# First layer's conditioning weights as the stationary operand in full precision, the input loaded first, modulation in two fused passes

## Chip, cores, metric

One of the cores of a Trainium2 chip runs the program. The metric is the device time of one launch in microseconds (us); the time before is 1392.67 us, the median of three runs (1392.63 to 1394.99).

## The reference, cut to what matters

A two-layer network over 512 latent tokens of 1024 channels, with 256 context tokens. Layer 0 is a bidirectional gated recurrence, layer 1 a convolution module. Both begin with a modulated RMSNorm whose shift and scale come from a conditioning vector:

```python
def _ada(cvec, w, b):                       # w is 1024 x 3072
    m = jax.nn.silu(cvec) @ w + b
    return jnp.split(m, 3, axis=-1)         # shift, scale, gate
def _modulate(x, g, shift, scale):
    return _rmsnorm(x, g) * (1 + scale) + shift
# layer 0
shift, scale, gate = _ada(c, ada_w[0], ada_b[0])
h = _modulate(x, norm_g[0], shift[:, None], scale[:, None])
shift_c, scale_c, gate_c = _ada(c_ctx, ada_w[0], ada_b[0])
hc = _modulate(ctx, norm_g[0], shift_c, scale_c)
y, yc = _hgrn2_mixer(h, hc, ...)            # first step: h @ w_in, hc @ w_in
```

## The kernel before, in words

Channels lie on the 128 partitions, in KD = 8 blocks (`k`), tokens along the free dimension (512 for `x`, 256 for the context). Large products take operands split into a high part in fp32r and a low part that is the rest (`split`, L134 to L142), and sum three products: high by high, high by low, low by high.

The change lies in the start, before the first head's work. `ada_start(jj)` (L144) computes shift and scale for two of the eight blocks of channels, for the latent and the context vector at once (two columns: `sc`, `sc4`). Each of the four calls takes four pieces of weights `ada{jj}_{kk}` of 128x2x512. As the table `ADA_SPLIT` (L36) says, a piece is either split (high part on ScalarE, low part on VectorE or GpSimd) and multiplied in fp32r, or multiplied whole in fp32. Here the vector is the stationary operand (2 or 4 columns) and the weights stream past it, 512 columns to a matmul (L150, L154, L156). The sums are rows `ps[0:4]`; they are copied (`adarow`, L158) and turned into columns by four small matmuls against `sel` (L161), and then `mod_s` and `mod_g` are made (L164, L165).

`rms_rstd` (L182) squares `x` on ScalarE, adds on VectorE and GpSimd, sums over partitions by a matmul with ones (L195) and gives the reciprocal root `rs`. Then `xn = x*rs` (L262) and `modulate` (L200): high part on ScalarE, the affine form again on VectorE (L202), their difference as the low part (L203). For the context the first multiplication is on GpSimd (L274).

`early_products` (L247) runs 24 matmuls for each of five first weight pieces `we0` to `we4` (L251 to L253, 120 in all), in steps as blocks of `h` come. The next work on TensorE is the product `pc` of the first weight piece with the context (L301).

Loads go on the SP queue in the order of the code (`load`, L90, keeps program order): four pieces of `ada` for each `jj`, `x` behind the first four, the weight pieces between them as `EARLY_LOADS` says, the context with `jj` = 2. The buffers of `ada` pieces (tag `araw`) are 6. In what order each engine issues its instructions is set by a scheduler at build time, from the dependences and an estimate of durations; a matmul of f32 operands stands in the trace as two records with a weight load each.

Of the kernel before, what the change touches and what calls it, by code (L numbers as in the profile page):

```python
# [35 lines left out]
ADA_SPLIT = ((1, 1, 1, 1), (1, 0, 2, 1), (1, 0, 2, 1), (1, 1, 0, 0))  # L36
EARLY, EARLY_LOADS, CTX_AT = 5, (3, 2, 0, 0), 2
# [23 lines left out]
def hybrid_kernel(ctx: ExitStack, tc: tile.TileContext, xT, ctxT, cvec, consts, norm_g, ada_b, ada_a, ada_c,  # L61
# [63 lines left out]
    sc4 = cpool.tile([P, KD, 4], F32R, name="sc4")  # L125
    V.tensor_copy(out=sc4[:, :, 0:2], in_=sc)
    V.tensor_tensor(out=sc4[:, :, 2:4], in0=sc, in1=sc4[:, :, 0:2].bitcast(F32), op=ALU.subtract)

# [15 lines left out]
    def ada_start(jj, raws, pool, sel):  # L144
        ps = ps_m.tile([P, 512], F32, name=f"adaps{jj}", tag="ms")
        n = 4 if ADA_SPLIT[jj][0] else 2
        for kk, raw in enumerate(raws):
            if not ADA_SPLIT[jj][kk]:
                for k in range(2):
                    mm(ps[0:2], lhsT=sc[:, 2 * kk + k, :], rhs=raw[:, k, :], start=(kk == 0 and k == 0), stop=(kk == 3 and k == 1))  # L150
                continue
            hi, lo = split(pool, raw, [2, 512], f"ada{jj}_{kk}", V if ADA_SPLIT[jj][kk] == 1 else G, ("ahi", "alo"), 2)
            for k in range(2):
                mm(ps[0:4], lhsT=sc4[:, 2 * kk + k, :], rhs=hi[:, k, :], start=(kk == 0 and k == 0), stop=False)  # L154
            for k in range(2):
                mm(ps[0:2], lhsT=sc4[:, 2 * kk + k, 0:2], rhs=lo[:, k, :], start=False, stop=(kk == 3 and k == 1))  # L156
        row = pool.tile([4, 512], F32, name=f"adarow{jj}", tag="adarow", bufs=2)
        V.tensor_copy(out=row[0:n], in_=ps[0:n])  # L158
        pt_ = ps_m.tile([P, 512], F32, name=f"adat{jj}", tag="ms")
        for i in range(4):  # L160
            mm(pt_[:, 2 * i:2 * i + 2], lhsT=row[0:n, i * P:(i + 1) * P], rhs=sel[0:n], start=True, stop=True)  # L161
        for i in range(2):
            j = 2 * jj + i
            V.tensor_scalar(out=mod_s[:, j, :], in0=pt_[:, 2 * i:2 * i + 2], scalar1=ab[:, 0, j:j + 1], scalar2=None, op0=ALU.add)  # L164
            V.tensor_scalar(out=mod_g[:, j, :], in0=pt_[:, 4 + 2 * i:6 + 2 * i], scalar1=ab1[:, j:j + 1],  # L165
                            scalar2=ng[:, 0, j:j + 1], op0=ALU.add, op1=ALU.mult)
# [33 lines left out]
    def modulate(t, k, gcol, scol, hi, lo):  # L200
        act(out=hi[k], in_=t, func=AF.Identity, scale=gcol, bias=scol)
        V.tensor_scalar(out=t, in0=t, scalar1=gcol, scalar2=scol, op0=ALU.mult, op1=ALU.add)  # L202
        V.tensor_tensor(out=lo[k], in0=t, in1=hi[k].bitcast(F32), op=ALU.subtract)  # L203
# [6 lines left out]
    # ================= layer 0: bidirectional gated recurrence =================  # L210
    with l0:
# [8 lines left out]
        with tc.tile_pool(name="pinit", bufs=1) as pi:  # L220
            mk = pi.tile([P, 5, P], F32, name="mk")
            eye = pi.tile([4, 4], F32, name="eye")
            nc.gpsimd.dma_start(out=eye, in_=consts[0:4, C_IDN:C_IDN + 4])
            sel = pi.tile([4, 2], F32, name="sel")
            V.tensor_tensor(out=sel, in0=eye[:, 0:2], in1=eye[:, 2:4], op=ALU.add)
            # loads in the order of their use: the vectors' weights, and the first products' between them
            wsrc = [w_in[2, 0, 0], w_in[3, 0, 0], w_in[2, 0, 1], w_in[0, 0, 0], w_in[0, 0, 1]]
            araws, wraws, todo = [], [], list(range(EARLY))
            for jj in range(4):
                araws.append([pi.tile([P, 2, 512], F32, name=f"ada{jj}_{kk}", tag="araw", bufs=6) for kk in range(4)])  # L230
                for kk in range(4):
                    load(araws[jj][kk], ada_a[jj, kk])
                if jj == 0:
                    for i in range(4):
                        load(x_sb[:, 2 * i:2 * i + 2, :], xT[:, 2 * i:2 * i + 2, :])
                for i in todo[:EARLY_LOADS[jj]]:
                    wraws.append(wpool.tile([P, KD, P], F32, name=f"we{i}_raw", tag="raw"))
                    load(wraws[i], wsrc[i])
# [43 lines left out]
            # lower bounds: softmax over the one layer, cumulative sum less the first  # L282
# [46 lines left out]
        def gla(h, j, sg, qs, v):  # L329
# [5 lines left out]
            # cumulative log decays within the chunks, forward and backward  # L335
# [3 lines left out]
            # decays from a context token to the context's end (forward) and start (backward)  # L339
# [16 lines left out]
            # the last head's state and operands lie where the context was  # L356
# [10 lines left out]
            # chunk totals and references; prefix and suffix sums of the totals by level  # L367
# [25 lines left out]
            # block decays  # L393
# [9 lines left out]
            # decayed queries and keys about each chunk's reference  # L403
# [11 lines left out]
            # state terms  # L415
# [21 lines left out]
            # scores by level, both directions at once  # L437
# [45 lines left out]
            # the first product opens the bank, and each later region's first overwrites what it finds  # L483
# [90 lines left out]
        for gi in range(8):  # L574
# [15 lines left out]
            else:  # L590
# [14 lines left out]
                # residual done: its squares and its scaled copy, then the next layer's normalised input  # L605
# [24 lines left out]
                # the transform of the convolution's taps  # L630
# [24 lines left out]
    # ================= layer 1: convolution module =================  # L655
    with ExitStack() as l1:
# [4 lines left out]
        # the convolution's transforms  # L661
# [10 lines left out]
        with tc.tile_pool(name="pu", bufs=1) as pu:  # L672
            for g in range(4):
# [3 lines left out]
                # one row of the grid to a tile: its high part on one half of the partitions, its low part on the other  # L677
# [62 lines left out]
        # LayerNorm over the channels: mean, then the squares about it  # L740
# [23 lines left out]
        # gate path, and the product with it  # L764
# [18 lines left out]
        # residual with the gated bias of the last projection  # L783
# [40 lines left out]
        for mq in range(4):  # L824
            # the last outputs by halves of the tokens, so that the first half is done while the second is summed
# [27 lines left out]
def _constants():  # L853
# [13 lines left out]
    # a depthwise convolution of one row as products between two transforms: the discrete Fourier  # L867
    # transform of NDFT points, in which the row, zeros after it, is as good as padded at both ends
# [9 lines left out]
    # real part p1 - p3, imaginary part p1 + p2  # L878
# [53 lines left out]
```

## Time and profile before

| | |
|---|---|
| median of three runs | 1392.67 us |
| the profiled execution's own span | 1389.6 us (its own time is this span; the runs' median has 3.1 us more around it) |
| TensorE busy | 1332.2 us, 96% of the span |
| VectorE, ScalarE, GpSimd busy | 962.8, 637.4, 368.9 us |
| first matmul of `pc` starts | 77.77 us |
| TensorE busy before that | 61.25 us |
| loads | 115.72 MB on the SP queue |

To read it: rows name engine, source line, operation, output<-inputs and shape. PE is TensorE's matmuls, PEld its weight loads (they run beside matmuls), DVE VectorE, ACT ScalarE, POOL GpSimd, SP the queue that issues loads. Matmuls overlap in their pipeline, so that the time between starts, not the length of a record, tells the pace. PEclk is the TensorE clock granted, as a share of 2.4 GHz; 0.5 is the level of 1.2 GHz.

### The profile page before, as it was taken

The page shows a single profiled execution, that of the slowest core. Times are in us where ns is not written, and L with a number is a line of the kernel's source. Part 1 is how long each engine was busy: PE and PEld are TensorE (multiplying, and loading weights), DVE is VectorE, ACT ScalarE, POOL GpSimd, SP SyncE. Part 2 cuts the span into 40 slices and gives each one's busy share as a digit, 9 for nine tenths or more (in the row PEclk, how much of TensorE's full clock was granted, in tenths as well). Part 3 has the DMA queues.
Part 4 walks back from the last instruction along what each step waited for, and adds up shares of the span by engine and source line. Part 5 has one row for each costly group of instructions (what it writes and reads, how often), then busy time and mean ns, then how long its engine had stood idle before and what let it go on. Part 6 is the DMA issues. An engine that isn't in the chain of part 4 may idle for free.

```text
span 1389.6 us, 18990 instructions
## 1 busy us (share of the span) xinstructions
PE 1332.2 (96%) x7530; PEld 1124.9 (81%) x7530; DVE 962.8 (69%) x1486; ACT 637.4 (46%) x965; POOL 368.9 (27%) x302
## 2 busy tenths in 40 slices
PE   6999999999999999999999999999999999986997
PEld 2588988998888898888898889867787877865887
DVE  8868787896687786787688777756656747278323
ACT  6455553562355354465345455443223333458321
POOL 3222241240240151140033133122211213267221
PEclk9999999999999999999999999999999999998999
DMA  9312113114112312212211312023422322120321
GB/s 361 123 61 77 46 62 107 61 46 146 67 46 64 120 46 88 75 51 92 92 46 47 122 46 75 28 79 106 136 92 91 108 89 92 64 76 28 124 89 61
DMA packets 35720, 119.05 MB, mean 86 GB/s; under 512 B 4562, under 2 KB 6898, under 8 KB 35632
## 3 DMA queue, kind: packets, MB, share of 16 engines
q1 hardware_dynamic: 34960, 115.72, 24.8%
q0 software_dynamic: 672, 2.13, 0.7%
q8 instruction: 59, 0.97, 0.3%
q14 instruction: 29, 0.24, 0.1%
HBM read 115.74 MB, written 2.10 MB: 85 GB/s over the span
## 4 chain that ended last, share of the span: by engine, by line
PE 61%; DVE 22%; ACT 5%; DMA 4%; POOL 4%; issue 3%; SPq 0%; DVEq 0%; ACTq 0%; POOLq 0%
PE pa L688 4%; PE pa L689 4%; PE pa L693 4%; PE pz L301 2%; PE pz L302 2%; PE pz L304 2%; PE pi L728 2%; PE cop L842 2%; PE cop L846 2%; PE cop L843 2%; PE op L530 2%; PE h_sc L465 2%; DVE adacc L176 2%; PE op L532 2%; PE op L531 2%
## 5 line engine op out<-in xcount | busy, mean ns | idle before, releaser
L688 PE MATMUL pa<-ci_hi,h_hi 128*128 128x512 f32 x256 | 99.6, 398 | 1.9 <-ACT h_hi L649 1.9
L689 PE MATMUL pa<-ci_lo,h_hi 128*128 128x512 f32 x256 | 100.4, 396 | 0.0
L116 POOL TENSOR_SCALAR sg<-sg 128x1536 f32<-128x1536 f32 x16 | 76.6, 4787 | 70.7 <-ACT sg L549 70.5
L301 PE MATMUL pz<-h_hi,wz_hi 128*128 128x512 f32 x232 | 93.3, 402 | 0.8 <-ACT wz_hi L139 0.8
L302 PE MATMUL pz<-h_lo,wz_hi 128*128 128x512 f32 x232 | 92.9, 401 | 0.0
L176 DVE SCALAR_TENSOR_TENSOR adacc<-adb,sc,adacc 128x128 f32<-128x128 f32 x224 | 82.0, 384 | 3.6
L141 POOL TENSOR_TENSOR ci_lo<-ci_raw,ci_hi 128x1024 fp32r<-128x1024 f32 x18 | 44.5, 2472 | 144.4 <-ACT ci_hi L139 124.6
L141 POOL TENSOR_TENSOR cg_lo<-cg_raw,cg_hi 128x1024 fp32r<-128x1024 f32 x16 | 62.2, 3889 | 66.9 <-PE pgt L774 28.2
L139 ACT ACTIVATE ci_hi<-ci_raw 128x1024 fp32r<-128x1024 f32 x29 | 30.7, 1059 | 93.8 <-PE pa L693 53.6
L693 PE MATMUL pa<-ci_hi,h_lo 128*128 128x512 f32 x224 | 72.1, 400 | 0.0
L312 PE MATMUL pv<-wv_hi,h_hi 128*128 128x256 f32 x256 | 64.8, 288 | 0.0
L313 PE MATMUL pv<-wv_hi,h_lo 128*128 128x256 f32 x256 | 64.1, 286 | 0.0
L400 POOL TENSOR_TENSOR h_f<-h_fac 128x16 f32<-128x16 f32 x16 | 10.0, 627 | 198.6 <-DVE h_kl L446 147.1
L304 PE MATMUL pz<-h_hi,wz_lo 128*128 128x512 f32 x232 | 61.3, 399 | 0.0
L432 DVE SCALAR_TENSOR_TENSOR h_S<-h_S,h_dec,h_kb 128x128 f32<-128x128 f32 x96 | 48.7, 507 | 18.0 <-ACT h_kb L426 16.9
L139 ACT ACTIVATE wz_hi<-wz_raw 128x1024 fp32r<-128x1024 f32 x29 | 30.7, 1057 | 64.6 <-DMA wz_raw<-in_w_in 51.7
L302 PE MATMUL pc<-hc,wz_hi 128*128 128x256 f32 x232 | 60.1, 291 | 0.0
L301 PE MATMUL pc<-hc,wz_hi 128*128 128x256 f32 x232 | 59.7, 289 | 0.0
L688 PEld LDWEIGHTS pa<-ci_hi,h_hi 128*128 128x128 f32 x256 | 48.2, 188 | 13.5 <-issue 2.7
L141 DVE TENSOR_TENSOR wz_lo<-wz_raw,wz_hi 128x1024 fp32r<-128x1024 f32 x29 | 35.4, 1222 | 32.3 <-ACT wz_hi L139 32.1
L689 PEld LDWEIGHTS pa<-ci_lo,h_hi 128*128 128x128 f32 x256 | 48.2, 188 | 11.3 <-issue 0.7
L377 POOL TENSOR_TENSOR h_ref<-h_tot,h_gt 128x64 f32<-128x64 f32 x16 | 17.5, 1091 | 146.4 <-DVE h_ref L404 136.7
(335 smaller groups left out, 4089.3 us busy)
## 6 DMA issues: line engine op xcount, KB each, us to landing
adb<-in_ada_c SPq DMA_DIRECT2D x32, 512.0 KB, 3.4
ci_raw<-in_c_in SPq DMA_DIRECT2D x32, 512.0 KB, 3.4
wz_raw<-in_w_in SPq DMA_DIRECT2D x29, 512.0 KB, 3.4
ada<-in_ada_a SPq DMA_DIRECT2D x16, 512.0 KB, 7.2
wv_raw<-in_w_v SPq DMA_DIRECT2D x16, 512.0 KB, 3.4
wg_raw<-in_w_in SPq DMA_DIRECT2D x16, 512.0 KB, 3.4
cg_raw<-in_c_gate SPq DMA_DIRECT2D x16, 512.0 KB, 3.5
co_raw<-in_c_out SPq DMA_DIRECT2D x16, 512.0 KB, 3.5
```

Of the source, the lines that this page charges most:

```text
L116: (G if pool_min else V).tensor_scalar(out=t, in0=t, scalar1=EMAX, scalar2=None, op0=ALU.min)
L139: act(out=hi, in_=raw, func=AF.Copy)
L141: lo_eng.tensor_tensor(out=lo, in0=raw, in1=hi.bitcast(F32), op=ALU.subtract)
L176: V.scalar_tensor_tensor(out=acc, in0=raw[:, k, :], scalar=sc[:, k, 0:1], in1=acc, op0=ALU.mult, op1=ALU.add)
L301: mm(ps[:, :T], lhsT=hi[:, k, :], rhs=rhi[k], start=(k == 0), stop=False)
L302: mm(ps[:, :T], lhsT=hi[:, k, :], rhs=rlo[k], start=False, stop=False)
L304: mm(ps[:, :T], lhsT=lo[:, k, :], rhs=rhi[k], start=False, stop=(k == KD - 1))
L312: mm(ps[:, :256], lhsT=lhi[k][:, c], rhs=hi[:, k % 4, :], start=(k == 0), stop=False)
L313: mm(ps[:, :256], lhsT=llo[k][:, c], rhs=hi[:, k % 4, :], start=False, stop=False)
L688: mm(pss[t], lhsT=h_hi[:, 2 * kq + k, c], rhs=hi[:, k, :], start=(kq == 0 and k == 0), stop=False)
L689: mm(pss[t], lhsT=h_hi[:, 2 * kq + k, c], rhs=lo[:, k, :], start=False, stop=False)
L693: mm(pss[t], lhsT=h_lo[:, 2 * kq + k, c], rhs=hi[:, k, :], start=False, stop=(kq == 3 and k == 1))
```

## The change

The pieces of `ada` weights become the stationary operand, in f32 and whole, in blocks of 128x128, and the vector `sc` (two columns) streams past. The sums come out as columns, so the splits, the row copy, the four small matmuls, `sel`, `sc4` and `ADA_SPLIT` go. `modulate` forms `x*mod_g*rs` in one VectorE pass, the high part on ScalarE, and the low part in a second VectorE pass; `xn` and the GpSimd multiplication go. `x` is loaded ahead of the first `ada` pieces, there are nine buffers for these, and `EARLY_LOADS` is (1, 2, 1, 1).

```diff
-ADA_SPLIT = ((1, 1, 1, 1), (1, 0, 2, 1), (1, 0, 2, 1), (1, 1, 0, 0))
-EARLY, EARLY_LOADS, CTX_AT = 5, (3, 2, 0, 0), 2
+EARLY, EARLY_LOADS, CTX_AT = 5, (1, 2, 1, 1), 2
...
-    def ada_start(jj, raws, pool, sel):
+    def ada_start(jj, raws):
         ps = ps_m.tile([P, 512], F32, name=f"adaps{jj}", tag="ms")
+        first = None
         for kk, raw in enumerate(raws):
...
             for k in range(2):
-                mm(ps[0:4], lhsT=sc4[:, 2 * kk + k, :], rhs=hi[:, k, :], start=(kk == 0 and k == 0), stop=False)
-            for k in range(2):
-                mm(ps[0:2], lhsT=sc4[:, 2 * kk + k, 0:2], rhs=lo[:, k, :], start=False, stop=(kk == 3 and k == 1))
-        row = pool.tile([4, 512], F32, name=f"adarow{jj}", tag="adarow", bufs=2)
-        V.tensor_copy(out=row[0:n], in_=ps[0:n])
...
+                for i in range(4):
+                    opens, ends = kk + k + i == 0, kk == 3 and k == 1 and i == 3
+                    with tc.issue_after(first.ins) if first else nullcontext():
+                        got = mm(ps[:, 2 * i:2 * i + 2], lhsT=raw[:, k, i * P:(i + 1) * P], rhs=sc[:, 2 * kk + k, :], start=opens, stop=ends)
+                    first = first or got
...
-    def modulate(t, k, gcol, scol, hi, lo):
-        act(out=hi[k], in_=t, func=AF.Identity, scale=gcol, bias=scol)
-        V.tensor_scalar(out=t, in0=t, scalar1=gcol, scalar2=scol, op0=ALU.mult, op1=ALU.add)
-        V.tensor_tensor(out=lo[k], in0=t, in1=hi[k].bitcast(F32), op=ALU.subtract)
+    def modulate(t, src, k, gcol, scol, r, hi, lo):
+        V.scalar_tensor_tensor(out=t, in0=src, scalar=gcol, in1=r, op0=ALU.mult, op1=ALU.mult)
+        act(out=hi[k], in_=t, func=AF.Identity, bias=scol)
+        V.scalar_tensor_tensor(out=lo[k], in0=t, scalar=scol, in1=hi[k].bitcast(F32), op0=ALU.add, op1=ALU.subtract)
...
-                araws.append([pi.tile([P, 2, 512], F32, name=f"ada{jj}_{kk}", tag="araw", bufs=6) for kk in range(4)])
-                for kk in range(4):
-                    load(araws[jj][kk], ada_a[jj, kk])
+                araws.append([pi.tile([P, 2, 512], F32, name=f"ada{jj}_{kk}", tag="araw", bufs=9) for kk in range(4)])
                 if jj == 0:
                     for i in range(4):
                         load(x_sb[:, 2 * i:2 * i + 2, :], xT[:, 2 * i:2 * i + 2, :])
+                for kk in range(4):
+                    load(araws[jj][kk], ada_a[jj, kk])
...
-                    V.tensor_tensor(out=t, in0=x_sb[:, k, :], in1=rs, op=ALU.mult)
-                    modulate(t, k, mod_g[:, k, 0:1], mod_s[:, k, 0:1], hx_hi, hx_lo)
+                    modulate(t, x_sb[:, k, :], k, mod_g[:, k, 0:1], mod_s[:, k, 0:1], rs, hx_hi, hx_lo)
...
-                    G.tensor_tensor(out=c_sb[:, k, :], in0=c_sb[:, k, :], in1=rc, op=ALU.mult)
-                    modulate(c_sb[:, k, :], k, mod_g[:, k, 1:2], mod_s[:, k, 1:2], hc_hi, hc_lo)
+                    modulate(c_sb[:, k, :], c_sb[:, k, :], k, mod_g[:, k, 1:2], mod_s[:, k, 1:2], rc, hc_hi, hc_lo)
```

TensorE from its first work, as it stood before (`adaps` sums the conditioning products, `adat` turns them, `rx_ss` sums the squares of `x`):

```order
L154 MATMUL adaps_184<-ada_0_hi,sc_106 4x512 x2
L156 MATMUL adaps_184<-ada_0_lo,sc_106 2x512 x2
L154 MATMUL adaps_184<-ada_1_hi,sc_106 4x512 x2
L156 MATMUL adaps_184<-ada_1_lo,sc_106 2x512 x2
L154 MATMUL adaps_184<-ada_2_hi,sc_106 4x512 x2
L156 MATMUL adaps_184<-ada_2_lo,sc_106 2x512 x2
L154 MATMUL adaps_184<-ada_3_hi,sc_106 4x512 x2
L156 MATMUL adaps_184<-ada_3_lo,sc_106 2x512 x2
L161 MATMUL adat_219<-sel,adarow_217 128x2 x4
L195 MATMUL rx_ss<-rx_sq_228,ones 128x512
L195 MATMUL rx_ss<-rx_sq_233,ones 128x512
L154 MATMUL adaps_280<-ada_0_hi,sc_106 4x512 x2
```

and now, up to the first early products (`pe`; each of the groups of eight is one piece of `ada` weights):

```order
L149 MATMUL adaps_177<-sc,ada_0_126 128x2 x8
L184 MATMUL rx_ss<-rx_sq_214,ones 128x512
L184 MATMUL rx_ss<-rx_sq_219,ones 128x512
L149 MATMUL adaps_177<-sc,ada_1_127 128x2 x8
L149 MATMUL adaps_177<-sc,ada_2_128 128x2 x8
L149 MATMUL adaps_177<-sc,ada_3_129 128x2 x8
L149 MATMUL adaps_254<-sc,ada_0_140 128x2 x8
L149 MATMUL adaps_254<-sc,ada_1_141 128x2 x8
L149 MATMUL adaps_254<-sc,ada_2_142 128x2 x8
L149 MATMUL adaps_254<-sc,ada_3_143 128x2 x8
L236 MATMUL pe_253<-h_hi,we_hi 128x512
L237 MATMUL pe_253<-h_lo,we_hi 128x512
```

The sum of squares stands between the first and the second piece, the whole of `jj` = 1 ahead of the first early product, and the products of a step follow each other by weight piece. Behind these stand 30 products, `rc_ss`, the last 32 small matmuls and 72 products, and then `pc`. From the first matmul of `pc` on, the rows of all five engines are the same as before, apart from buffer numbers and a few loads on SP near this point.

SP's queue as it began before:

```order
L91 DMA ada_0_133<-in_ada_a 128x1024
L91 DMA ada_1_134<-in_ada_a 128x1024
L91 DMA ada_2_135<-in_ada_a 128x1024
L91 DMA ada_3_136<-in_ada_a 128x1024
L91 DMA x_sb<-in_xT 128x1024 x4
L91 DMA we_raw<-in_w_in 128x1024 x3
L91 DMA ada_0_151<-in_ada_a 128x1024
L91 DMA ada_1_152<-in_ada_a 128x1024
```

and now:

```order
L90 DMA x_sb<-in_xT 128x1024 x4
L90 DMA ada_0_126<-in_ada_a 128x1024
L90 DMA ada_1_127<-in_ada_a 128x1024
L90 DMA ada_2_128<-in_ada_a 128x1024
L90 DMA ada_3_129<-in_ada_a 128x1024
L90 DMA we_raw<-in_w_in 128x1024
L90 DMA ada_0_140<-in_ada_a 128x1024
```

`x` has moved ahead of the `ada` pieces, and two of the first three weight pieces behind those of `jj` = 1.

VectorE now, between the first and the second step's modulation (`rc_sq` are the context's squares, `we_lo` the low part of the fourth weight piece):

```order
L136 TENSOR_TENSOR we_lo<-we_raw,we_hi 128x1024
L178 TENSOR_TENSOR rc_sq_407<-rc_sq_407,rc_sq_409 128x256
L178 TENSOR_TENSOR rc_sq_407<-rc_sq_407,rc_sq_412 128x256
L178 TENSOR_TENSOR rc_sq_407<-rc_sq_407,rc_sq_415 128x256
L178 TENSOR_TENSOR rc_sq_407<-rc_sq_407,rc_sq_418 128x256
L178 TENSOR_TENSOR rc_sq_407<-rc_sq_407,rc_sq_421 128x256
L178 TENSOR_TENSOR rc_sq_407<-rc_sq_407,rc_sq_424 128x256
L178 TENSOR_TENSOR rc_sq_407<-rc_sq_407,rc_sq_427 128x256
L153 TENSOR_SCALAR mod_s<-adaps_254,ab 128x2
```

The second step's `mod_s` stands behind the seven additions for the context, which before stood between the second and third step's.

## Rows read from the trace of the kernel before

**Rows 1.** The page, its first two parts: busy time of the engines; the span in 40 slices of 34.7 us, TensorE's busy tenths and its granted clock.

```profile
PE 1332.2 (96%) x7530; PEld 1124.9 (81%) x7530; DVE 962.8 (69%) x1486; ACT 637.4 (46%) x965; POOL 368.9 (27%) x302
...
PE   6999999999999999999999999999999999986997
...
PEclk9999999999999999999999999999999999998999
```

**Rows 2.** Busy time by stretch, before and after the first matmul of `pc`. Columns: stretch in us, its length, then busy us (instructions) of PE, PEld, DVE, ACT, POOL, granted clock, DMA share, GB/s.

```profile
0.00:77.77 77.77, 61.25 (x222) 32.16 (x222) 59.99 (x106) 40.08 (x61) 20.81 (x23) 0.93 0.57 216
77.77:1389.60 1311.83, 1270.99 (x7308) 1092.77 (x7308) 902.84 (x1381) 597.31 (x905) 348.06 (x279) 0.99 0.24 78
```

**Rows 3.** The timeline of all engines at the hand-over to `pc`. Columns: start, length in us, then the group; in brackets idle time before and what ended it.

```profile
77.12 1.57 ACT L547 ACTIVATE sg<-pe 128x512 f32<-128x512 f32 x3 [6.07 <-PE pe L253]
...
77.77 0.38 PE L301 MATMUL pc<-hc,we_hi 128*128 128x256 f32 x1 [0.74 <-ACT sg L547]
```

**Rows 4.** Waits that TensorE's path goes through in the start, from the timeline.

```profile
23.75 1.01 PE L156 MATMUL adaps<-ada_lo,sc 128*2 128x512 f32 x2 [2.65 <-DVE ada_lo L141]
...
39.47 1.05 PE L161 MATMUL adat<-sel,adarow 4*128 4x2 f32 x8 [2.54 <-DVE adarow L158]
...
55.35 1.53 ACT L201 ACTIVATE h_hi<-xn,mod_s,mod_g 128x512 fp32r<-128x512 f32 x2 [3.67 <-DVE mod_g L165]
```

**Rows 5.** Landings, from the timeline: ScalarE's first use of the first and of the twelfth 512 KB piece in SP's order.

```profile
4.93 1.06 ACT L139 ACTIVATE ada_hi<-ada 128x1024 fp32r<-128x1024 f32 x1 [1.65 <-DMA ada<-in_ada_a]
...
19.38 1.06 ACT L139 ACTIVATE ada_hi<-ada 128x1024 fp32r<-128x1024 f32 x1 [0.28 <-DMA ada<-in_ada_a]
```

**Rows 6.** TensorE's conditioning groups, by line and form: count, busy us, mean ns of one, idle before and what ended it.

```profile
L150 PE MATMUL adaps<-ada,sc 128*2 128x512 f32 x16 | 9.6, 742 | 0.0
...
L156 PE MATMUL adaps<-ada_lo,sc 128*2 128x512 f32 x24 | 9.1, 468 | 3.1 <-DVE ada_lo L141 2.9 <-DVE sel L225 0.2
L154 PE MATMUL adaps<-ada_hi,sc 128*4 128x512 f32 x24 | 8.6, 443 | 6.3 <-ACT ada_hi L139 6.0 <-DVE mod_g L165 0.3
...
L161 PE MATMUL adat<-sel,adarow 4*128 4x2 f32 x32 | 4.2, 249 | 3.3 <-DVE adarow L158 3.3
```

**Rows 7.** Timeline of TensorE at the upper level: 32 records of f32 matmuls, each with a 118x128 weight load and 64 columns; then early products.

```profile
1023.72 3.68 PE L728 MATMUL pi<-tr,pr 118*128 118x64 f32 x32
...
48.37 0.39 PE L251 MATMUL pe<-h_hi,we_hi 128*128 128x512 f32 x1
48.60 0.39 PE L252 MATMUL pe<-h_lo,we_hi 128*128 128x512 f32 x1
48.83 0.39 PE L253 MATMUL pe<-h_hi,we_lo 128*128 128x512 f32 x1
49.06 0.40 PE L251 MATMUL pe<-h_hi,we_hi 128*128 128x512 f32 x1
```

**Rows 8.** Timeline at the lower level: the sum of squares of `x` (PE) and one of its weight loads; two weight loads of 256-column matmuls; last, two f32 weight loads at the upper level.

```profile
17.09 3.54 PE L195 MATMUL rx_ss<-rx_sq,ones 128*128 128x512 f32 x4 [2.95 <-DVE rx_sq L189]
...
18.07 0.34 PEld L195 LDWEIGHTS rx_ss<-rx_sq,ones 128*128 128x128 f32 x1 [0.52 <-issue]
...
141.54 0.33 PEld L301 LDWEIGHTS pc<-hc,wz_hi 128*128 128x128 f32 x1
141.76 0.33 PEld L302 LDWEIGHTS pc<-hc,wz_hi 128*128 128x128 f32 x1
...
54.80 0.30 PEld L195 LDWEIGHTS rc_ss<-rc_sq,ones 128*128 128x128 f32 x2
```

**Rows 9.** Busy time and granted clock by stretch (columns as in the second group): pairs of a stretch and the one behind it, and one alone.

```profile
136.54:139.95 3.41, 1.39 (x11) 1.20 (x11) 1.85 (x2) 1.92 (x3) 0.00 (x0) 0.97 0.01 5
139.95:143.36 3.41, 3.41 (x19) 3.41 (x19) 1.94 (x4) 2.32 (x4) 0.76 (x1) 0.53 0.46 154
419.85:423.26 3.41, 1.86 (x14) 1.61 (x13) 2.02 (x4) 3.41 (x7) 0.00 (x0) 0.97 0.45 154
423.26:426.67 3.41, 3.41 (x18) 3.31 (x17) 3.41 (x7) 2.43 (x6) 0.00 (x0) 0.53 0.02 5
1023.78:1027.20 3.42, 3.42 (x33) 3.42 (x32) 1.92 (x2) 1.46 (x2) 0.00 (x0) 1.00 0.14 22
1027.20:1030.60 3.40, 3.40 (x18) 2.83 (x18) 1.32 (x4) 0.69 (x1) 0.00 (x0) 1.00 0.36 137
1235.62:1239.04 3.42, 1.75 (x8) 1.08 (x6) 3.21 (x3) 2.36 (x4) 2.06 (x2) 1.00 0.00 0
```

**Rows 10.** VectorE, ScalarE and GpSimd groups that the change takes out or replaces, by line and form; first the fused pass as layer 1 already has it (L650).

```profile
L650 DVE SCALAR_TENSOR_TENSOR h_lo<-xg,adac,h_hi 128x512 fp32r<-128x512 f32 x8 | 5.4, 740 | 0.0
...
L141 DVE TENSOR_TENSOR ada_lo<-ada,ada_hi 128x1024 fp32r<-128x1024 f32 x10 | 14.4, 1436 | 3.9 <-ACT ada_hi L139 3.7
...
L262 DVE TENSOR_TENSOR xn<-x_sb,rx_sq 128x512 f32<-128x512 f32 x8 | 7.2, 940 | 0.0
...
L203 DVE TENSOR_TENSOR h_lo<-xn,h_hi 128x512 fp32r<-128x512 f32 x8 | 5.9, 750 | 0.0
...
L202 DVE TENSOR_SCALAR xn<-xn,mod_g,mod_s 128x512 f32<-128x512 f32 x8 | 4.2, 541 | 1.1 <-ACT h_hi L201 1.1
...
L139 ACT ACTIVATE ada_hi<-ada 128x1024 fp32r<-128x1024 f32 x12 | 12.5, 1052 | 5.1 <-DMA ada<-in_ada_a 3.1 <-PE adaps L154 1.3 <-issue 0.6
...
L274 POOL TENSOR_TENSOR c_sb<-c_sb,rc_sq 128x256 f32<-128x256 f32 x8 | 6.8, 886 | 20.1 <-ACT rc_sq L197 20.1
```

More of the change, by code (lines that the diff above doesn't have):

```diff
@@ L123, in hybrid_kernel @@
     V.tensor_tensor(out=sc, in0=sc, in1=cv, op=ALU.mult)
-    sc4 = cpool.tile([P, KD, 4], F32R, name="sc4")
-    V.tensor_copy(out=sc4[:, :, 0:2], in_=sc)
-    V.tensor_tensor(out=sc4[:, :, 2:4], in0=sc, in1=sc4[:, :, 0:2].bitcast(F32), op=ALU.subtract)
     mod_s = cpool.tile([P, KD, 2], F32, name="mod_s")
@@ L142, in split @@
         return hi, lo
-    def ada_start(jj, raws, pool, sel):
+    def ada_start(jj, raws):
         ps = ps_m.tile([P, 512], F32, name=f"adaps{jj}", tag="ms")
-        n = 4 if ADA_SPLIT[jj][0] else 2
+        first = None
         for kk, raw in enumerate(raws):
-            if not ADA_SPLIT[jj][kk]:
-                for k in range(2):
-                    mm(ps[0:2], lhsT=sc[:, 2 * kk + k, :], rhs=raw[:, k, :], start=(kk == 0 and k == 0), stop=(kk == 3 and k == 1))
-                continue
-            hi, lo = split(pool, raw, [2, 512], f"ada{jj}_{kk}", V if ADA_SPLIT[jj][kk] == 1 else G, ("ahi", "alo"), 2)
-            for k in range(2):
-                mm(ps[0:4], lhsT=sc4[:, 2 * kk + k, :], rhs=hi[:, k, :], start=(kk == 0 and k == 0), stop=False)
-            for k in range(2):
-                mm(ps[0:2], lhsT=sc4[:, 2 * kk + k, 0:2], rhs=lo[:, k, :], start=False, stop=(kk == 3 and k == 1))
-        row = pool.tile([4, 512], F32, name=f"adarow{jj}", tag="adarow", bufs=2)
-        V.tensor_copy(out=row[0:n], in_=ps[0:n])
-        pt_ = ps_m.tile([P, 512], F32, name=f"adat{jj}", tag="ms")
-        for i in range(4):
-            mm(pt_[:, 2 * i:2 * i + 2], lhsT=row[0:n, i * P:(i + 1) * P], rhs=sel[0:n], start=True, stop=True)
+            for k in range(2):
+                for i in range(4):
[3 more added lines that the diff above has]
+                    first = first or got
         for i in range(2):
             j = 2 * jj + i
-            V.tensor_scalar(out=mod_s[:, j, :], in0=pt_[:, 2 * i:2 * i + 2], scalar1=ab[:, 0, j:j + 1], scalar2=None, op0=ALU.add)
-            V.tensor_scalar(out=mod_g[:, j, :], in0=pt_[:, 4 + 2 * i:6 + 2 * i], scalar1=ab1[:, j:j + 1],
+            V.tensor_scalar(out=mod_s[:, j, :], in0=ps[:, 2 * i:2 * i + 2], scalar1=ab[:, 0, j:j + 1], scalar2=None, op0=ALU.add)
+            V.tensor_scalar(out=mod_g[:, j, :], in0=ps[:, 4 + 2 * i:6 + 2 * i], scalar1=ab1[:, j:j + 1],
                             scalar2=ng[:, 0, j:j + 1], op0=ALU.add, op1=ALU.mult)
@@ L221, in hybrid_kernel @@
             mk = pi.tile([P, 5, P], F32, name="mk")
[L222 to L225, printed above, removed]
             wsrc = [w_in[2, 0, 0], w_in[3, 0, 0], w_in[2, 0, 1], w_in[0, 0, 0], w_in[0, 0, 1]]
@@ L256, in hybrid_kernel @@
             for jj in range(4):
-                ada_start(jj, araws[jj], pi, sel)
+                ada_start(jj, araws[jj])
                 if jj == 0:
```

## The prediction, made blind

> **What bounds the kernel now.** Read first the page's totals and slices [rows 1]: TensorE is busy 96% of the span, and the first slice of 34.7 us stands at six tenths, where the next 34 are at nine. So time can come out of this kernel in the start, and hardly elsewhere. The stretch view cuts the span where the first product of the context, `pc`, starts [rows 2]: before 77.77 us TensorE is busy 61.25 us, behind it 1270.99 of 1311.83. From `pc` on every engine issues what it issued before, so I take the 1311.8 us behind it as they are and ask one thing: when does `pc` start? At the hand-over it starts 0.65 us after ScalarE takes up the last early products [rows 3]. That is the term that ends my sum.
>
> What made 77.77 so late are waits of TensorE on VectorE and ScalarE [rows 4]: 2.65 us for a low part of the weights, 2.54 us for the row copy `adarow`, and 3.67 us in which ScalarE waited for `mod_g`. Loads were no better at first: in SP's order the first 512 KB piece was used at 4.93 and the twelfth, which ScalarE waited for, at 19.38 [rows 5], 1.31 us a piece.
>
> **What goes.** The splits: 14.4 us on VectorE, 12.5 us on ScalarE, two low parts on GpSimd; the row copies; GpSimd's 6.8 us for the context [rows 10]. Modulation loses `xn` (7.2 us) and the affine pass (4.2 us) and gains, for each block, one more fused pass like the one layer 1 has (0.74 us, where the plain subtraction took 0.75). All of it lies beside TensorE; what it gives is that TensorE no longer waits for it, so I book it at nothing itself and let TensorE run without those waits. TensorE loses 24 + 24 + 16 records of 512 columns and 32 small ones, 31.5 us of overlapping records [rows 6].
>
> **What comes.** Each of the four steps is now 32 f32 matmuls, 64 records, each with a full weight load and two columns. The nearest row is the inverse transform's run [rows 7]: 32 such records with 64 columns in 3.68 us, 0.115 us each, with the weight load as the pace. So a step costs 64 x 0.115 = 7.4 us at the upper clock level, all on TensorE's path. At the lower level no row shows a load without columns to hide in; one f32 weight load takes 0.34 us there against 0.19 (two in 0.30, overlapping) above, and loads of 256-column matmuls follow at 0.214 us [rows 8]. I take 0.214, as these are whole loads that follow one another; below it can't be under 0.115, above I allow twice 0.115 = 0.23.
>
> **The clock** decides. I book the work up to the sum of squares at the lower level, as that sum was after a thin stretch (four records in 3.54 us [rows 8]); at the upper one it would be half. After thin stretches it falls back [rows 9]: with TensorE busy 1.39 of 3.41 us, and with 1.86, the next 3.41 us are granted 0.53; after such a dense stretch the level is the upper one again. Against this, the stretch at 1023.78 is full of loads with 64 columns each, and the clock stays at 1.00 in the next. The new steps are longer than any thin stretch here, have a load at the same pace as those, but put through a thirty-second of their columns. Neither row settles it. Busy time alone doesn't sort them: the stretch at 1235.62 has 1.75 us and stays at 1.00, that at 419.85 has 1.86 and is followed by a fall. I go by resemblance in what is put through, and take the fall.
>
> The Trainium skill (TensorE: Matmul & The Clock Gate, "What's actually happening") says that a monitor sets the clock by how busy the engine has been lately; by that rule an engine that issues without a gap keeps the upper level. The run at 1023.78 agrees, the pair at 419.85 and 1235.62 doesn't; by the rule the sum would be that of rival 1.
>
> **The sum, with the fall.** `x` now comes first, so the first weight piece is the fifth: 4.93 + 4 x 1.31 = 10.2 us. Its 16 records at 0.214: 13.6. Squares and additions of `x` end by then, since they start at 4.93 instead of 10.5; the sum of squares at the lower level: 17.1. The other 48 records and the 64 of the second step, 112 x 0.214 = 24.0: 41.1. Early products stand 0.23 us apart [rows 7]: 18 are 4.1, and 3.4 us of them at the lower level lose 1.7: 46.9. Third step: 3.4 us at the upper level (30 records), 34 at 0.214 = 7.3, together 10.7: 57.6. 30 products and the context's sum (a quarter of 3.54, halved: 0.4), with 1.7 lost: 66.6. Fourth step 10.7: 77.3. 72 products, 16.6 + 1.7: 95.6. Hand-over 0.65: `pc` at 96.3 instead of 77.8, **18.5 us later**. The profiled execution's 1389.6 becomes 1408.1, and since the runs' median lies 3.1 above it, 1411.2.
>
> What hides the rest: `mod_s` of the second step now stands behind the context's additions on VectorE, which need the 22nd piece (4.93 + 21 x 1.31 = 32.4, and some 3 us of work), ready by 37 and needed at 57.6. SP waits before the loads of the fourth step until pieces of the second are read (about 38), and behind these are the fifth weight piece, the constants and the masks, whose cast stands ahead of the third `mod_s`; four pieces more put it at 45, before the 57.6 of its step. The last modulation has 42 products (9.7 us) before it in TensorE's order, and costs under 5 us on VectorE and ScalarE. So DMA and VectorE are not late in this case.
>
> Bounds: the lower pace at 0.23 adds 196 x 0.016 = 3.1; a fall at a step's start adds 30 x 0.1 = 3 us each in two steps, one that comes 3.4 us later takes as much off. This case's own range is 1405 to 1417.
>
> **Rival 1, the other side: the clock stays up** once raised. Point of decision: whether steps of loads with two columns keep the level. Then: 17.1 as above, 112 x 0.115 = 12.9: 30.0; 4.1: 34.1; 7.4: 41.5; 7.3: 48.8; 7.4: 56.2; 16.6: 72.8; `pc` at 73.4, 4.3 us earlier: 1388.4. If already the first 16 records raise it, the sum of squares halves: 1386.6. For it speaks the stretch at 1023.78. In this case the masks (about 42) come a little behind the third step (41.5), but 30 products cover that.
>
> **Rival 2: the clock falls, but loads keep their pace** of 0.115 at both levels. Then only products pay: 12.0, 15.5, 28.4, 34.2, 41.6, 50.6, 58.0, 76.3, `pc` at 77.0: 1391.9, no change. The 0.34 against 0.19 of one load speaks against it. The Trainium skill (same page, "LDWEIGHTS") gives a load's time by its columns over 1.2 GHz and names no clock level; by it 128 columns are 0.107 us, an estimate, which the 0.115 at the upper level bears out; no run here shows it at the lower.
>
> **Chances.** The forecast 0.63, rival 1 0.26, rival 2 0.11. About 0.2% (2.8 us) can be told from no change. Rival 1 lies 1.5 to 3.3 us beyond that line and I give 0.02 of it to no change: faster 0.24, same 0.13, slower 0.63. The range leaves out the dearest part of the forecast and the cheapest of rival 1: 1387 to 1416; the forecast's own is 1405 to 1417.
>
> **What would show it.** In the profile after: `pc` near 96 us; in the steps of `ada` matmuls a granted clock of about 0.5 and records 0.2 us apart, 0.115 in the parts at 1.0; the early products behind each step starting at half pace; no wait of TensorE on VectorE or ScalarE beyond 1 us before `pc`; the stretch behind `pc` 1311.8 us long within 3. Wrong it is if the clock holds 1.0 through a step (rival 1), if records stand 0.115 us apart at 0.5 (rival 2), or if TensorE waits for a load or for VectorE inside a step, which would mean that I misjudged what is hidden.

## The result: slower by 9 us

The changed kernel takes 1401.7 us, median of 4 runs (1400.2 to 1403.67), against 1392.65 for the kernel before (1392.13 to 1394.99): a ratio of 1.0068, interval 1.0051 to 1.0085. The forecast was 1411: of the 18.5 us that it added, 9.0 came. 1401.7 lies in the stated range (1387 to 1416), which was widened to take in rival 1, and below the forecast's own (1405 to 1417). The mechanism that it took is in the trace; two terms of the sum were off, and both made it too dear: the start of `pc`, by 2.4 us, and the stretch behind it, by 6.6 us. In the profiled executions: 16.1 us more up to `pc`, 6.6 us less behind it, 1399.1 us for 1389.6.

### The profile after

The totals, the slices and the granted clock, against [rows 1]: TensorE's clock, 9 throughout the first slices before, is 7 and 6 in the first two.

```profile
PE 1345.3 (96%) x7690; PEld 1166.1 (83%) x7690; DVE 935.4 (67%) x1461; ACT 623.3 (45%) x953; POOL 357.9 (26%) x291
...
PE   7999998999999999999999999999999999986997
...
PEclk7699999999999999999999999999999999998999
```

The two stretches, against [rows 2]: up to the first product of `pc`, and behind it. Columns: stretch in us, its length, busy us (instructions) of TensorE, granted clock, DMA share, GB/s.

```profile
0.00:93.85 93.85, 82.68 (x382) 0.76 0.46 179
93.85:1399.10 1305.25, 1262.62 (x7308) 0.99 0.24 78
```

`pc` starts 16.1 us later (93.85 for 77.77) with TensorE busy 82.68 instead of 61.25 us before it, at a mean clock of 0.76 instead of 0.93. But the same 7308 matmuls behind it need 1305.25 us, where they took 1311.83.

TensorE's waits before `pc`, all of them (us in total, times, longest), and the hand-over, against [rows 4] and [rows 3]. All of the waits on VectorE are gone. The one before the first record is for a load, and ends at 10.4 us (10.2 in the sum):

```profile
PE adaps L149 <- DMA ada<-in_ada_a: 10.4, 1, 10.4
PE pc L284 <- ACT sg L530: 0.7, 1, 0.7
```

```profile
93.20 1.58 ACT L530 ACTIVATE sg<-pe 128x512 f32<-128x512 f32 x3 [14.81 <-PE pe L238]
...
93.85 0.38 PE L284 MATMUL pc<-hc,we_hi 128*128 128x256 f32 x1 [0.74 <-ACT sg L530]
```

What TensorE does instead, from its timeline (start, length, group): the records of the conditioning steps (L149), the sum of squares and the first and last early products of two runs.

```profile
10.44 3.54 PE L149 MATMUL adaps<-sc,ada 128*128 128x2 f32 x16 [10.44 <-DMA ada<-in_ada_a]
13.84 3.38 PE L184 MATMUL rx_ss<-rx_sq,ones 128*128 128x512 f32 x4
17.06 21.10 PE L149 MATMUL adaps<-sc,ada 128*128 128x2 f32 x112
38.02 0.77 PE L236 MATMUL pe<-h_hi,we_hi 128*128 128x512 f32 x1
...
43.28 0.63 PE L236 MATMUL pe<-h_hi,we_hi 128*128 128x512 f32 x1
43.71 0.55 PE L237 MATMUL pe<-h_lo,we_hi 128*128 128x512 f32 x1
44.09 0.39 PE L238 MATMUL pe<-h_hi,we_lo 128*128 128x512 f32 x1
44.32 0.39 PE L236 MATMUL pe<-h_hi,we_hi 128*128 128x512 f32 x1
...
45.02 11.45 PE L149 MATMUL adaps<-sc,ada 128*128 128x2 f32 x64
...
65.98 8.78 PE L149 MATMUL adaps<-sc,ada 128*128 128x2 f32 x64
...
74.62 0.77 PE L236 MATMUL pe<-h_hi,we_hi 128*128 128x512 f32 x1
```

The first 16 records take 3.4 us, 0.213 us each, not 0.115 [rows 7], and from 20.4 to 37.9 us they stand 0.213 us apart as well (mean of some 80 start-to-start times in the trace). In two parts they are faster: 0.112 from 17.06 to 20.3 and from 66 to 71.4. Behind each step the products first stand 0.43 us apart (43.28, 43.71), then 0.23 (44.09, 44.32). The same stretches cut where the level changes, TensorE busy, instructions, clock:

```profile
17.06:20.33 3.27, 3.27 (x31) 0.97 1.03 421
20.33:38.02 17.69, 17.69 (x85) 0.50 0.98 383
38.02:44.22 6.20, 6.20 (x16) 0.52 0.95 359
44.22:47.63 3.41, 3.41 (x29) 0.97 0.43 154
47.63:56.34 8.71, 8.71 (x43) 0.50 0.01 2
56.34:61.29 4.95, 4.95 (x13) 0.52 0.00 0
61.29:71.53 10.24, 10.24 (x72) 0.99 0.00 0
71.53:78.35 6.82, 6.82 (x25) 0.51 0.00 0
78.35:93.85 15.50, 14.77 (x64) 1.00 0.00 1
```

Read a row as a pair: TensorE is busy 17.69 of 17.69 us and is granted 0.50, the lower of the two levels (1.2 GHz); in the row above it the clock is 0.97 and the records come at 0.112 us. Then the early products, which come through at half pace, bring the clock back at 44.22; the next step loses it again at 47.63. Before each of these falls TensorE was at records of two columns, before each of the later rises at products of 512.

### The profile page after: what moved, and what is told of

It is laid out like the page before. It is cut to its first block, busy times and chain, and to the rows that moved or that the text cites. A ratio compares the mean times of both kernels' runs of the same rounds, so it can differ in the third digit from the quotient of the medians.

```text
span 1399.1 us, 19233 instructions
## 1 busy us (share of the span) xinstructions
PE 1345.3 (96%) x7690; PEld 1166.1 (83%) x7690; DVE 935.4 (67%) x1461; ACT 623.3 (45%) x953; POOL 357.9 (26%) x291
## 4 chain that ended last, share of the span: by engine, by line
PE 62%; DVE 21%; ACT 6%; DMA 4%; POOL 4%; issue 3%; SPq 0%; DVEq 0%; ACTq 0%; POOLq 0%
PE pa L671 4%; PE pa L672 4%; PE pa L676 4%; PE adaps L149 3%; PE pz L284 2%; PE pz L285 2%; PE pi L711 2%; PE pz L287 2%; PE cop L825 2%; PE cop L826 2%; PE cop L829 2%; DVE adacc L165 2%; PE h_sc L448 2%; DVE h_S L415 2%; PE pgt L757 2%
## 5 line engine op out<-in xcount | busy, mean ns | idle before, releaser
L415 DVE SCALAR_TENSOR_TENSOR h_S<-h_S,h_dec,h_kb 128x128 f32<-128x128 f32 x96 | 51.6, 538 | 16.1 <-ACT h_kb L409 15.0
```

The source lines that it names most:

```text
L415: V.scalar_tensor_tensor(out=S[:, d, dst, :], in0=S[:, d, src, :], scalar=dec[:, d, db:db + 1], in1=kb[:, d, pb * P:(pb + 1) * P], op0=ALU ...
```

## The experiments

Two questions: is it the little that goes through the array that lowers the clock, and why is the stretch behind `pc` shorter, although every engine issues there what it issued before? A third is what the hidden parts, modulation and load order, are worth.

The change takes out `sc4`, a tile of 128 bytes per partition. All tiles behind it in its pool, and all weight tiles, lie 128 bytes lower since then (the first high part of a weight piece at 80768 instead of 80896 of a partition, in the compiled program); `h_hi` (32896) and `h_lo` (49280) stay. That these places set the pace is theory P. Each kernel below was timed beside runs of the kernel before on the same chip (median 1392.65 to 1393.68); ratios are to these.

### 1. The kernel before, profiled again

No edit.

> The kernel before, unchanged, profiled once more beside the others. Question: behind the first pc product the profile of after needed 6.6 us less than the profile of before (1305.25 us against 1311.83), with pa products 0.2276 us apart instead of 0.2327 and pgt products 0.2274 instead of 0.2327. Theory P (place of the tiles in SBUF: without sc4 every tile behind it in its pool and every weight tile lies 128 bytes lower): this profile shows again 0.2327 for pa and pgt and about 1311.8 us behind the first pc. Rival Q (the two profiles were taken on different occasions, and the spacing belongs to the occasion): 0.2275 and about 1305 to 1307 us.

Measured: 1391.8 us, ratio 0.999 (0.9974 to 1.0007). Its two stretches; then the convolution's input products, from the first `pa` to the last (1019 intervals):

```profile
0.00:77.91 77.91, 61.79 (x222) 0.93 0.56 216
77.91:1389.90 1311.99, 1270.80 (x7308) 0.99 0.24 78
938.03:1161.30 223.27, 223.27 (x1020) 0.99 0.32 102
```

The stretch behind `pc` is 1311.99 us again, and `pa` products stand 0.2325 us apart in this profile, 0.2327 in the first: the difference belongs to the kernels, not to the occasion. Rival Q falls.

### 2. After, with the place of `sc4` filled

```
+    pad = cpool.tile([P, KD, 4], F32, name="pad")
+    G.memset(pad[:, 0, 0:1], 0.0)
```

> After, with an unused tile of 128 bytes per partition where sc4 stood, so that the tiles behind it lie where the kernel before has them; the order of the instructions stays. Theory P: pa and pgt 0.2327 us apart again, about 1311 us behind the first pc, total about 1401.7 + 5 to 6.6 = 1406.7 to 1408.3 us. Rival Q: 0.2275 us, about 1305 us behind the first pc, total 1401.7 us.

Measured: 1409.32 us, ratio 1.0121 (1.0089 to 1.0154), where after has 1.0068 (1.0051 to 1.0085): 7 us more in the median with an unused tile. The profiled execution is the longest of its four (1411.97). The two stretches, the `pa` stage, and the 112 records behind the sum of squares:

```profile
0.00:97.39 97.39, 85.78 (x382) 0.89 0.46 173
97.39:1410.00 1312.61, 1272.08 (x7308) 0.99 0.24 78
958.05:1181.44 223.39, 223.39 (x1019) 0.99 0.32 102
...
17.83:41.59 23.76, 23.76 (x114) 1.00 0.90 334
```

Behind `pc` 1312.61 us, 7.4 more than in after. P holds. `pc` itself starts at 97.39, 3.5 us later than in after, and this is not the tile's place: here the level did not come up after the sum of squares, as it did in after at 17.06 to 20.33. The pace tells it: the 112 records stand 0.213 us apart and the products behind them 0.427, up to 47.7 us, as in after at 0.50. The clock column reads 1.00 there, and 0.89 in the first row; it seems to stand at 1.00 until the profile has a first change of level. Kernels 5 and 7 below, placed as after is, have no rise there either (23.75 us for the 112 records), while 6 and 8 have one. Where the level rises differs even between two profiles of one kernel (the first step's products come to full pace at 44.09 in after and at 41.77 in 8), and `pc` starts between 93.85 and 97.39 in the six profiles with records of two columns.

### 3. The kernel before, with `sc4` in another pool

```
-    sc4 = cpool.tile([P, KD, 4], F32R, name="sc4")
+    sc4 = p0.tile([P, KD, 4], F32R, name="sc4")
```

> The kernel before, with sc4 alone taken from another pool, so that the tiles behind its old place lie 128 bytes lower, as in after; nothing else changes. Theory P: pa and pgt 0.2275 us apart, 5 to 6.6 us less behind the first pc, total about 1392.7 - 5 to 6.6 = 1386.1 to 1387.7 us. Rival Q: 1392.7 us, the same spacing as in the kernel before on this chip.

Measured: 1387.95 us, ratio 0.9967 (0.9952 to 0.9982), a gain of 4.6 us by moving one tile.

```profile
0.00:77.35 77.35, 61.09 (x223) 0.91 0.57 217
77.35:1381.70 1304.35, 1262.17 (x7308) 0.99 0.24 78
936.04:1153.97 217.93, 217.93 (x1019) 1.00 0.32 104
```

The `pa` stage takes 217.93 us at a clock of 1.00, where the first profile of before has 221.81 at 1.00: 3.9 us over 1019 products. So P works on the kernel before as well, by itself.

### 4. After, with 128 columns in each record

```
-  got = mm(ps[:, 2 * i:2 * i + 2], lhsT=..., rhs=sc[:, 2 * kk + k, :], ...)
+  got = mm(ps[:, W * i:W * i + W], lhsT=..., rhs=cut(sc, 2 * (2 * kk + k), [[0, W // 2], [1, 2]]), ...)   # W = 128
```

> After, with 128 moving columns in each of the records of the conditioning layer instead of 2 (the two columns repeated 64 times, of which two are used). Theory F (the granted clock falls in these steps because a record of 2 columns gives the array little to do; with more columns it stays up): clock 1.0 through the four steps, although each record does 64 times the work; records about 0.12 to 0.23 us apart (0.115 is the load alone, 0.23 would be what 128 columns in f32 cost if they ran at the rate of the f32 rx_ss record, 512 columns in 0.85 us), first pc at about 74 to 94 us, total 1380 to 1402 us. Rival G (the f32 weight loads themselves, or waits between them, bring the clock down): clock 0.5 in the steps again, records 0.21 us apart or more (up to 0.45), first pc at 94 us or later, total 1402 us or more.

Measured: 1379.29 us, ratio 0.9907 (0.9875 to 0.994), faster than both kernels. TensorE's timeline of the steps and the stretches:

```profile
11.01 3.75 PE L149 MATMUL adaps<-sc,ada 128*128 128x128 f32 x16 [11.01 <-DMA ada<-in_ada_a]
14.56 2.63 PE L184 MATMUL rx_ss<-rx_sq,ones 128*128 128x512 f32 x4
17.02 12.67 PE L149 MATMUL adaps<-sc,ada 128*128 128x128 f32 x112
...
33.67 7.31 PE L149 MATMUL adaps<-sc,ada 128*128 128x128 f32 x64
```

```profile
0.00:72.82 72.82, 61.07 (x383) 1.00 0.59 231
72.82:1378.20 1305.38, 1263.40 (x7308) 0.99 0.24 78
17.02:29.45 12.43, 12.43 (x114) 1.00 1.04 411
```

F holds and G falls: the same weight loads with 64 times the columns run at 1.00, 112 records in 12.43 us, 0.112 us apart. The first 16 records (3.75 us) and the start of the sum of squares are still slow; after that the level does not fall before `pc`. `pc` starts at 72.82 instead of 93.85. That is the price of the clock in this change: 21.0 us. The total lies a little under the expected 1380 to 1402, and `pc` under the expected 74 to 94, since the 128 columns cost nothing beside the loads.

### 5 to 8. What counts in the place

```
5:  +    pad0 = cpool.tile([P, KD, 4], F32, name="pad0")   # ahead of x_sb
6:  +    pad0 as in 5, and pad as in 2
7:  +    pad = cpool.tile([P, KD, 8], F32, name="pad")     # where sc4 stood
8:  after, unchanged
```

> After, with an unused tile of 128 bytes per partition ahead of the first tile, so that every tile, the moving inputs h_hi and h_lo with the weights, lies 128 bytes higher. The weights stand where the kernel before has them (80896, a multiple of 256), the inputs no longer (33024 and 49408, multiples of 256 too). Theory R (what counts is where the weights lie against the moving input): as after, pa and pgt 0.2275 us apart, about 1305 us behind the first pc, total as after. Theory A (what counts is the weights' own address): as with the tile at the place of sc4, 0.2327 us apart, about 1311 us behind the first pc, some 5 to 6.6 us over after.

> After, with unused tiles of 128 bytes per partition at both places: the inputs h_hi and h_lo 128 bytes higher (33024, 49408), the weights 256 bytes higher (81024, not a multiple of 256, as in after). Theory R: slow spacing, pa and pgt 0.2327 us, about 1311 us behind the first pc, 5 to 6.6 us over after. Theory A: fast spacing, 0.2275 us, total as after.

> After, with an unused tile of 256 bytes per partition where sc4 stood: the inputs where they are in after, the weights 256 bytes higher. If the places repeat every 256 bytes, both theories R and A expect the spacing of after (0.2275 us, about 1305 us behind the first pc, total as after); if what counts is that the weights lie lower by 128 bytes than in the kernel before, or something that changes with a longer period, 0.2327 us or another value.

> After, unchanged, once more beside the three kernels with moved tiles, as their common base: first pc at about 93.9 us, about 1305 us behind it, pa and pgt 0.2275 us apart, 9 us over before.

Measured, with the kernels above; places are modulo 256 bytes, spacings are means of the start-to-start times of `pa` and `pgt` products (`pgt` are the convolution's gate products) in the trace:

| kernel | h_hi, h_lo at | weights at | pa, us | pgt, us | behind pc, us | ratio to before |
|---|---|---|---|---|---|---|
| before, 1 | 128 | 0 | 0.2325 | 0.2327 | 1311.99 | 0.999 (0.9974 to 1.0007) |
| 2 | 128 | 0 | 0.2326 | 0.2328 | 1312.61 | 1.0121 (1.0089 to 1.0154) |
| 6 | 0 | 128 | 0.2325 | 0.2328 | 1309.79 | 1.0087 (1.0066 to 1.0109) |
| after, 8 | 128 | 128 | 0.2276 | 0.2274 | 1305.80 | 1.0064 (1.0045 to 1.0084) |
| 5 | 0 | 0 | 0.2277 | 0.2275 | 1306.22 | 1.0067 (1.0043 to 1.009) |
| 7 | 128 | 128 (+256) | 0.2277 | 0.2274 | 1306.47 | 1.0067 (1.0046 to 1.0088) |
| 3 | 128 | 128 | 0.2276 | 0.2274 | 1304.35 | 0.9967 (0.9952 to 0.9982) |

R holds, A falls. A product of 512 columns is 5 ns dearer where its stationary and its moving tile lie 128 bytes apart modulo 256, and neither address matters alone. It does not matter which is which: in `pa` the input is the stationary operand, in `pgt` the weights are. The groups by line show it as well (busy us, mean ns of one), first kernel 5, then 6:

```profile
L676 PE MATMUL pa<-ci_hi,h_lo 128*128 128x512 f32 x224 | 70.9, 395 | 0.0
L755 PE MATMUL pgt<-h_lo,cg_hi 128*128 128x512 f32 x128 | 50.6, 396 | 0.0
```

```profile
L676 PE MATMUL pa<-ci_hi,h_lo 128*128 128x512 f32 x224 | 72.0, 400 | 0.0
L755 PE MATMUL pgt<-h_lo,cg_hi 128*128 128x512 f32 x128 | 51.4, 402 | 0.0
```

In the totals 6 lies 3.4 us over 8 (1405.75 against 1402.34), less than the 5 to 6.6 expected, and their intervals overlap; in the traces it is 4.0 us behind `pc`, 3.7 of it in the `pa` stage (223.26 against 219.52 us, both at 0.99). The rest of the 6.6 us is in layer 0 and varies more: from `pc` to the first `pa` 860.1 and 860.7 us in 1 and 2, 858.9 in 6, 858.0 to 858.3 in 8, 5 and 7; in the first two profiles, before and after, it is 862.3 and 857.2, which is 5.1 of their 6.6 us. Short falls of the clock (3.4 us at 0.50) add to this: one at the start of the `pa` stage makes it 1.6 us longer (219.52 us in 8 with it, 217.93 in 3 without). So the place is worth 4.0 us in the closest pair (6 and 8), and up to 7.6 in others (1 and 3), of which some 1.6 are such a fall. Behind `pa` nothing is left of the `pgt` products' gain (384 x 0.005 = 2 us): TensorE waits part of it, 0.5 us, for GpSimd's low parts, 13.0 us instead of 12.5 (the idle time before the group and what ended it), first in 1, then in 8:

```profile
L774 PE MATMUL pgt<-h_hi,cg_lo 128*128 128x512 f32 x128 | 38.0, 434 | 12.5 <-POOL cg_lo L141 12.5
```

```profile
L757 PE MATMUL pgt<-h_hi,cg_lo 128*128 128x512 f32 x128 | 37.8, 432 | 13.0 <-POOL cg_lo L136 13.0
```

### 9 to 12. The hidden parts, on the wide kernel

Here the start is some 21 us shorter than in after, so a cover that is too thin would show. The wide kernel again (9), with before's modulation, its product with rstd and three passes (10), with `x` behind the first four weight pieces (11), with the readout's tiles moved (12):

```
10: -  V.scalar_tensor_tensor(out=t, in0=src, scalar=gcol, in1=r, op0=ALU.mult, op1=ALU.mult)
    +  V.tensor_tensor(out=t, in0=x_sb[:, k, :], in1=rs, op=ALU.mult)
    +  G.tensor_tensor(out=c_sb[:, k, :], in0=c_sb[:, k, :], in1=rc, op=ALU.mult)
11: +  for kk in range(4): load(araws[jj][kk], ada_a[jj, kk])
       if jj == 0: ...   (x's four loads)
    -  for kk in range(4): load(araws[jj][kk], ada_a[jj, kk])
12: +  pad = pt.tile([P, 48], F32, name=f"{n}_pad", tag="pad", bufs=1)   # ahead of h_oh
```

> After with 128 moving columns in the records of the conditioning layer, once more, as the base of the three kernels beside it: first pc at about 72.8 us, about 1305 us behind it, total about 1380 us, 0.991 of before.

> The wide kernel with the modulation of before: the product with rstd as an instruction of its own (VectorE for x, GpSimd for the context), then one ScalarE and two VectorE passes. My prediction had the fused modulation hidden: 0 us, first pc at 72.8 us as in the wide kernel. Rival: with the start of layer 0 some 21 us shorter the cover is gone, and the eight products with rstd on GpSimd and the longer VectorE passes make the early products or the first pc wait: 1 to 6 us.

> The wide kernel with x loaded behind the first four weight pieces again, nothing else changed. Theory: TensorE gets its first weights some 2.5 us sooner (8.5 instead of 11 us) but then waits for the squares of x, which come some 3 us later (rx_ss at about 17.3 us as in before, instead of 14.6), and the records of the second step have to wait behind rx_ss on its queue: first pc 1 to 4 us later, at 74 to 77 us. Rival (the records behind rx_ss go ahead of it, or fill the gap): first pc within 1 us, 72 to 74 us.

> The wide kernel with an unused tile of 192 bytes ahead of the readout's tiles h_oh and h_ol (the stationary operand of the output projection), which alone move: from 192 modulo 256 to 128 modulo 256, where the moving weights wo stand. Theory R: the spacing of the op products falls from 0.2297 to about 0.227 us, as for pa, pgt and pg; with some 340 of them that is 0.9 us, less than the total can show. Theory A or no such rule for op: 0.2297 us as before.

Measured: 1380.58 us for 9 (0.9912, 0.9887 to 0.9936), 1380.29 for 10 (0.9914, 0.9884 to 0.9943), 1378.01 for 11 (0.989, 0.9859 to 0.9922), 1379.74 for 12 (0.9902, 0.9878 to 0.9926).

Modulation (10): hidden, `pc` at 72.85 against 72.47, and TensorE's only waits before it are still the first load and the hand-over. The rival falls: the fusing gives nothing here, and takes nothing.

Load order (11): both expectations were wrong. The timeline of TensorE:

```profile
5.03 9.68 PE L149 MATMUL adaps<-sc,ada 128*128 128x128 f32 x64 [5.03 <-DMA ada<-in_ada_a]
17.71 1.98 PE L184 MATMUL rx_ss<-rx_sq,ones 128*128 128x512 f32 x4 [3.00 <-DVE rx_sq L178]
19.53 7.31 PE L149 MATMUL adaps<-sc,ada 128*128 128x128 f32 x64
```

The first record starts at 5.03 instead of 10.48, the sum of squares then waits 3.00 us for the squares; 5.45 - 3.00 = 2.45, and `pc` starts at 69.99 instead of 72.47. TensorE has 64 records to do ahead of that wait, where in 9 it has 16. So loading the input first costs 2.5 us in the wide kernel, by the one profile of 11; the four others (4, 9, 10, 12) have `pc` at 72.4 to 72.9. The totals (1378.01 and 1380.58) can't tell this apart. The profile of 11 is of its fastest execution (1373.8, the slowest took 1381.05) and 3.5 us shorter behind `pc` too (1302.01 against 1305.53). Of these, 1.6 are in the `pa` stage (217.94 against 219.52): 9 has a fall of the clock at its start (0.50 from 930.68 to 934.09) and 11 has none. The rest stays open. In after itself, with the first records at the lower level, this was not tried.

Place (12): the expectation names the roles the wrong way round (`wo` is stationary in `op`, `h_oh` moves), which changes nothing in it. `op` products over `h_oh` and `h_ol` stood 0.2296 us apart in 9 and stand 0.2274 in 12, as R has it. The weights lay 64 bytes below them, modulo 256, and lie level now; in kernel 3, where they lay 64 above, it is 0.2332. First 9, then 12:

```profile
L513 PE MATMUL op<-h_oh,wo_hi 128*128 128x512 f32 x112 | 44.6, 398 | 0.0
L515 PE MATMUL op<-h_oh,wo_lo 128*128 128x512 f32 x112 | 44.6, 398 | 0.0
```

```profile
L514 PE MATMUL op<-h_oh,wo_hi 128*128 128x512 f32 x112 | 44.2, 395 | 0.0
L516 PE MATMUL op<-h_oh,wo_lo 128*128 128x512 f32 x112 | 44.3, 395 | 0.0
```

## Why the prediction was right, and where not

**The clock: right, and the term of 18.5 us came out at 16.1.** The early products behind a step come up to pace and the next step's records lose it, as the sum has it. Step by step, from the timeline: first piece at 10.44 (said 10.2); the sum of squares starts at 13.84 (13.6) and ends at 17.06 (17.1). The 112 records took 21.0 us and not 24.0: the level was up from 17.06 to 20.33, which I had allowed the third and fourth step and not this one. The 18 products took 7.0 and not 5.8, since the lower level held 6.2 us into them and not 3.4. Third step 11.3 (10.7), products and the context's sum 9.6 (9.0), fourth step 8.6 (10.7), the rest 19.2 (18.95). Together 2.4 us less. That is no more than such profiles differ by: in 2, 5 and 7, where the level did not come up, the 112 records took 23.75 us, and `pc` starts at 97.39, 94.88 and 95.13. A record at the lower level costs 0.213 us, I took 0.214. There was luck in this: the row behind it [rows 8] is of matmuls of 256 columns, in which the columns may set the pace as well as the loads, so it could not promise more than the bounds of 0.115 and 0.23.

**Rival 1 was the right sum for another kernel.** It had `pc` at 73.4 if the clock stays up, and with 128 columns, where it stays up, `pc` starts at 72.82. So the terms of the sum were sound, and the whole sign hung on the clock. The Trainium skill (TensorE: Matmul & The Clock Gate, "What's actually happening") sets the clock by how busy the engine has been; in after TensorE is busy 17.69 of 17.69 us at a clock of 0.50, and in kernel 4 12.43 of 12.43 at 1.00. With busy read as the profile's busy time, as the prediction read it, the trace does not agree, and the measurement decides: resemblance in what is put through [rows 9] was the better guide.

**Rival 2 falls:** loads do pay for the clock, 0.213 us against 0.112. The Trainium skill (TensorE: Matmul & The Clock Gate, "LDWEIGHTS") gives 0.107 us for 128 columns, an estimate from its rule: the trace agrees at the upper level and not at the lower.

**What was booked at nothing was nothing:** TensorE's waits before `pc` are two, the first load and the hand-over; the old modulation costs the same (10). Loading `x` first I had booked as the end of a wait; in the wide kernel it ends 3.00 us of waiting and delays the first record by 5.45.

**The step that failed** is "from `pc` on every engine issues what it issued before, so I take the 1311.8 us behind it as they are". The premise holds, the conclusion does not: the stretch took 1305.25 us, 6.6 less and beyond the 3 us that the prediction itself allowed, because the removed tile moved the weights to the inputs' place modulo 256 (short falls of the clock, 1.6 us for one in the `pa` stage, blur the size). With the place restored (2) the stretch is 1312.61 us (1311.8 in the forecast). That `pc` comes near there too (97.39 for 96.3), and the total with it (1409.32 for 1411.2), is chance: the late start comes of the rise that 2 lacks, and 5 and 7, placed as after is, lack it too. In after: 1411.2 - 2.4 - 6.6, and 0.5 as its median lies 2.6 above its profiled span and not 3.1, is 1401.7.

**What stays open:** by what path in the chip the places of two tiles set the pace of a matmul; no run here shows it, only that the offset counts, and not which tile has which.

## What to carry to other kernels

A busy TensorE is not a fast one: where weights become the stationary operand for a handful of columns, look at the pace of the records and at the granted clock, and try repeating the columns, which cost nothing here and gave 21 us. A tile that is added or removed moves all that lie behind it: before a few us are put down to an edit, put an unused tile in its place and run again, and look whether the clock fell at the same points in both profiles. And a sum from a trace tells when a stage can start; that the stage then takes as long as before is an assumption like any other.

## What the runs showed of the hardware that was not expected

- Matmuls of 128x128 weights by 512 columns follow each other at 0.227 us where the stationary and the moving tile have the same address modulo 256 bytes, and at 0.2325 where they differ by 128 (`pa` and `pgt`, every kernel here); by 64 it is 0.2296 or 0.2332, by the sign (`op`). In this kernel of 1390 us it is worth 4.0 us in the closest pair of profiles and 6.6 between before and after.
- The clock falls under a TensorE that never idles: records of two columns from 20.33 to 38.02 us at 0.50, without a gap. With 128 columns in the same records it stays at 1.00, and a record costs 0.112 us instead of 0.213: 64 times the columns in half the time.
- The granted clock in the profile reads 1.00 in stretches whose pace is that of the lower level, as long as the profile shows no change of level before them: in kernel 2 up to 47.7 us, with records 0.213 us apart.
